# The even block's depthwise convolution as a blockwise real Fourier transform on TensorE, and S5's GpSimd products on VectorE

## The chip, the cores and the metric

The kernel runs on one core of one Trainium2 chip. The metric is the device time of one execution in microseconds (us): the median of several runs. Traces and profile pages come from one further, profiled execution each. TensorE is called PE in the profile's rows (its weight loads PEld), VectorE DVE, ScalarE ACT, GpSimd POOL and SyncE SP.

## The reference

The program is a stack of blocks on 512 tokens of 1024 channels. The change touches only the first one, the even block. After a root-mean-square norm `u` of the input it computes:

```python
p = u @ ev_w_in                                  # 1024 -> 5120
a_in, a_z, b_val, b_gate, b_z = split(p)         # 1024 channels each
ya = gelu(s5_layer(a_in))                        # state-space layer, 64 groups of 16 channels
ya = ya * sigmoid(ya @ s5_w_glu + b_glu) * silu(a_z)
h  = b_val * sigmoid(b_gate)
h  = causal depthwise convolution of h, 31 taps, + conv_b
h  = silu(layer_norm(h))
yb = (h @ conv_w_pw + b_pw) * silu(b_z)
x  = x + rms_norm(concat(ya, yb) @ ev_w_out)
```

All of it is in float32. Products on TensorE are made in three passes of a high and a low part: high by high, low by high, high by low (`passes`, L271 to L273). The halves come from `split`: a copy on ScalarE gives the high part (L227), a subtraction the low part (L230).

## The kernel before, in words

The even block lasts from the start to about 728 us. Channels lie on the 128 partitions, 512 tokens along them. `linear` makes one block of 128 output channels at a time: one weight load by DMA (`wraw`), one copy (`whi`, ACT L227), one subtraction (`wlo`, L230), 24 matmuls of 128x512 into a bank of PSUM (`mm`, three banks), and an epilogue. There are two buffers each for `whi` and `wlo`. The order of instructions on each engine isn't the order of the code: this block alone is built under a scheduler that runs at build time, estimates durations and fixes the order of every engine. On the chip each engine then follows its own list strictly, and waits where a semaphore isn't there yet.

The stages, as the trace shows them:

- **Input blocks and tables** (22 to about 85 us): eight blocks of `a_in`, whose `wlo` subtractions GpSimd makes (`eng=nc.gpsimd`), and S5's tables on VectorE.
- **S5 groups** (`s5_group`, to about 200 us): eight groups of eight. For every pair of S5 groups VectorE makes products and sums (L685, L687, L693, L695), GpSimd two of the products (L686, L694); TensorE transposes and multiplies (L700, L701, L709), beside the 16 blocks of `a_z` and `b_z` and some blocks of the convolution's value and gate.
- **Scan** (`s5_scan`, about 204 to 372 us): 63 steps of four operations of 128x128 on VectorE (L743 to L746). Each step needs the one before; within a step L743 and L744 are free of each other, L745 needs L743, and L746 needs both sums.
- **Convolution**: eight blocks of channels, three ways. Four blocks on ScalarE and GpSimd: for each tap ScalarE scales a shifted copy (L853) and GpSimd adds it (L854). Two on TensorE with diagonal weights, which VectorE builds (L825, 62 high and 62 low tiles). Two on VectorE, one `scalar_tensor_tensor` per tap (L860), held back by hand until the scan's last step. The results go to DRAM (`cv_dr`).
- **Chunks and outputs** of S5 (L731, L761), each 128 small matmuls; the outputs need the scan's last state.
- **glu** (eight blocks, after gelu L903 and splits), with LayerNorm over channels on the reloaded convolution (`layer_norm_apply`) beside it, its silu (L919), the eight pointwise blocks, and the output matrix (16 blocks, to 692 us). Then the block's norm and the next block's first operations.

Of the kernel before, what the change touches and what calls it, by code (L numbers as in the profile page):

```python
# [735 lines left out]
def s5_scan(K, tb, rot, H):  # L736
# [3 lines left out]
    for c in range(1, 64):  # L740
        a = rot.tile([128, 2, G5], F32, name="sa")
        b = rot.tile([128, 2, G5], F32, name="sb")
        tt(out=a, in0=H[:, c - 1], in1=tb["R8"], op=OP.mult)  # L743
        tt(out=b, in0=H[:, c - 1, ::-1], in1=tb["J8"], op=OP.mult)  # L744
        tt(out=a, in0=H[:, c], in1=a, op=OP.add)  # L745
        last = tt(out=H[:, c], in0=a, in1=b, op=OP.add)  # L746
    return last
# [22 lines left out]
def stage_even(K, xt):  # L770
# [9 lines left out]
    with ExitStack() as es:  # L780
        R = pool(es, "evr", 2)
        uh, ul = K.enter(xt, K.rms_pre("norm_pre0"))
        K.xs.close()

# [25 lines left out]
        acc = K.stat("acc")  # L810
        first = []

        def conv_pe(j, hb, c):

            hs = [PE.tile([128, T + 30], F32R, name=n) for n in ("hbh", "hbl")]
            wt = [PE.tile([128, 31], F32R, name=n) for n in ("wth", "wtl")]
            K.split(wt[0], wt[1], K.v("conv_w", j, 241)[:, ::8], eng=nc.gpsimd)
            K.split(hs[0], hs[1], hb, eng=nc.gpsimd)
            ps = K.mm_ps()
            for q0 in range(0, 31, 8):  # L820
                n = min(8, 31 - q0)
                dg = [PE.tile([128, 8, 128], F32R, name=s, bufs=2) for s in ("dgh", "dgl")]
                for a, b in zip(dg, wt):
                    for q in range(n):
                        nc.vector.tensor_scalar(out=a[:, q], in0=K.ident, scalar1=b.bitcast(F32)[:, q0 + q:q0 + q + 1],  # L825
                                                scalar2=None, op0=OP.mult)
                K.passes(ps, [(dg[0][:, q], dg[1][:, q], hs[0][:, q0 + q:q0 + q + T], hs[1][:, q0 + q:q0 + q + T])
                              for q in range(n)], q0 == 0, q0 + n == 31)
            act(out=c, in_=ps, func=AF.Identity, bias=K.v("conv_b", j))

        def conv(j):
            kind = "p" if j in CONV_POOL else "e" if j in CONV_PE else "v"
            P = R if kind == "p" else PE
            hb = P.tile([128, T + 30], F32, name="hb" + kind, bufs=1 if kind == "e" else 2)
            nc.gpsimd.memset(hb[:, 0:30], 0.0)
            sg = R.tile([128, T], F32, name="sg")

            def epi_g(_, ps):
                act(out=sg, in_=ps, func=AF.Sigmoid)

            def epi_v(_, ps):
                nc.vector.tensor_tensor(out=hb[:, 30:], in0=ps, in1=sg, op=OP.mult)

            K.linear(w, [24 + j], uh, ul, epi_g)
            K.linear(w, [16 + j], uh, ul, epi_v)
            c = P.tile([128, T], F32, name="cvt" + kind, bufs=1 if kind == "e" else 2)
            if j in CONV_PE:
                conv_pe(j, hb, c)
            elif j in CONV_POOL:
                act(out=c, in_=hb[:, 0:T], func=AF.Identity, scale=K.v("conv_w", j), bias=K.v("conv_b", j))  # L850
                for q in range(1, 31):
                    t = R.tile([128, T], F32, name="cq")
                    act(out=t, in_=hb[:, q:q + T], func=AF.Copy, scale=K.v("conv_w", 8 * q + j))  # L853
# [1410 lines left out]
```

## Time and profile before

| | before |
|---|---|
| time, median of 3 runs | 4395.85 us (4386.81 to 4398.39) |
| profiled execution | 4396.65 us, span 4394.9 us, mean granted clock 0.967 |
| TensorE busy | 4106.9 us, 93% |
| VectorE busy | 2749.7 us, 63% |
| ScalarE busy | 1754.1 us, 40% |
| GpSimd busy | 766.1 us, 17% |

Rows of the profile read so: line of the kernel, engine, operation, output<-inputs, partitions x elements, count, then busy time and mean ns of one, then the idle time of the engine just ahead of them and what ended it. Rows of a timeline begin with the start and the duration in us. A matmul's recorded duration holds its whole way through the array; the distance between two starts is what TensorE needs for one.

### The profile page before, as it was taken

The page shows a single profiled execution, that of the slowest core. Times are in us where ns is not written, and L with a number is a line of the kernel's source. Part 1 is how long each engine was busy: PE and PEld are TensorE (multiplying, and loading weights), DVE is VectorE, ACT ScalarE, POOL GpSimd, SP SyncE. Part 2 cuts the span into 40 slices and gives each one's busy share as a digit, 9 for nine tenths or more (in the row PEclk, how much of TensorE's full clock was granted, in tenths as well). Part 3 has the DMA queues.
Part 4 walks back from the last instruction along what each step waited for, and adds up shares of the span by engine and source line. Part 5 has one row for each costly group of instructions (what it writes and reads, how often), then busy time and mean ns, then how long its engine had stood idle before and what let it go on. Part 6 is the DMA issues. An engine that isn't in the chain of part 4 may idle for free.

```text
span 4394.9 us, 54853 instructions
## 1 busy us (share of the span) xinstructions
PE 4106.9 (93%) x20700; PEld 3395.0 (77%) x20700; DVE 2749.7 (63%) x5196; ACT 1754.1 (40%) x2785; POOL 766.1 (17%) x746
## 2 busy tenths in 40 slices
PE   7877897999999898999999999999989999999998
PEld 5666676777876687888888888888877788877887
DVE  8999735545453799887665444444546878834334
ACT  3643634443335532444222232323264344444333
POOL 4765201101021333000000000000123222211000
PEclk9988998999999999999999999999999999999999
DMA  5553533334321123456654333434234222343222
GB/s 150 111 125 116 173 103 121 124 106 144 124 69 46 65 78 124 183 206 227 192 193 136 120 122 118 128 115 130 88 125 145 68 71 71 96 143 109 96 97 86
DMA packets 275064, 532.37 MB, mean 121 GB/s; under 512 B 75968, under 2 KB 149568, under 8 KB 271184
## 3 DMA queue, kind: packets, MB, share of 16 engines
q1 hardware_dynamic: 263328, 505.75, 36.4%
q10 hardware_dynamic: 9216, 9.97, 0.8%
q0 software_dynamic: 2256, 13.17, 0.7%
q8 instruction: 162, 2.65, 0.3%
q14 instruction: 102, 0.84, 0.1%
HBM read 438.11 MB, written 90.70 MB: 120 GB/s over the span
## 4 chain that ended last, share of the span: by engine, by line
PE 54%; DVE 11%; issue 3%; ACT 2%; DMA 1%; POOL 1%; DVEq 0%; POOLq 0%; SPq 0%; ACTq 0%
PE mm L271 15%; PE mm L272 15%; PE mm L273 15%; PE ax L1508 3%; PE z L1225 1%; DVE ti L1435 1%; DVE wlo L230 1%; PE ck L2033 1%; DVE ts L1433 1%; DVE bi L1451 1%; DVE wz L1985 0%; DVE bs L1449 0%; PE po L1234 0%; PE z L1207 0%; DVE eq L1463 0%
## 5 line engine op out<-in xcount | busy, mean ns | idle before, releaser
L271 PE MATMUL mm<-uh,whi 128*128 128x512 f32 (+1 forms) x2888 | 1152.0, 400 | 55.3 <-ACT uh L227 23.7
L273 PE MATMUL mm<-uh,wlo 128*128 128x512 f32 (+1 forms) x2888 | 1130.2, 392 | 56.3 <-DVE wlo L230 55.1
L272 PE MATMUL mm<-ul,whi 128*128 128x512 f32 (+1 forms) x2888 | 1130.7, 392 | 11.2 <-DVE ul L230 8.7
L230 DVE TENSOR_TENSOR wlo<-wraw,whi 128x1024 fp32r<-128x1024 f32 x416 | 530.5, 1277 | 520.1 <-ACT whi L227 509.7
L227 ACT ACTIVATE whi<-wraw 128x1024 fp32r<-128x1024 f32 x455 | 480.2, 1057 | 913.5 <-PE mm L272 655.1
L273 PEld LDWEIGHTS mm<-uh,wlo 128*128 128x128 f32 x2888 | 560.4, 194 | 171.7 <-DVE wlo L230 63.7
L271 PEld LDWEIGHTS mm<-uh,whi 128*128 128x128 f32 x2888 | 560.8, 195 | 170.3 <-ACT whi L227 25.9
L272 PEld LDWEIGHTS mm<-ul,whi 128*128 128x128 f32 x2888 | 560.9, 194 | 121.3 <-DVE ul L230 13.7
L272 PE MATMUL mm<-pl,vh 128*128 128x512 f32 (+1 forms) x1056 | 405.8, 384 | 0.3 <-DVE pl L230 0.3
L271 PE MATMUL mm<-ph,vh 128*128 128x512 f32 (+1 forms) x1056 | 394.2, 385 | 7.4 <-ACT ph L227 7.4
L273 PE MATMUL mm<-ph,vl 128*128 128x512 f32 (+1 forms) x1056 | 398.4, 384 | 0.0
L227 ACT ACTIVATE vh<-wraw 128x1024 fp32r<-128x1024 f32 x128 | 132.8, 1058 | 533.1 <-PE mm L272 327.4
L230 DVE TENSOR_TENSOR vl<-wraw,vh 128x1024 fp32r<-128x1024 f32 x128 | 155.4, 1223 | 206.1 <-ACT vh L227 206.1
L1605 DVE TENSOR_TENSOR Y<-mm,Y 128x512 f32<-128x512 f32 (+1 forms) x256 | 164.9, 670 | 142.3 <-PE mm L273 142.2
L1610 POOL COPY acc<-xt 128x256 f32<-128x256 f32 x2 | 1.9, 958 | 1430.7 <-DVE xt L1608 1430.7
L271 PEld LDWEIGHTS mm<-ph,vh 128*128 128x128 f32 x1056 | 200.0, 190 | 47.0 <-ACT ph L227 8.0
L272 PEld LDWEIGHTS mm<-pl,vh 128*128 128x128 f32 x1056 | 199.8, 189 | 39.5 <-DVE pl L230 0.5
L273 PEld LDWEIGHTS mm<-ph,vl 128*128 128x128 f32 x1056 | 199.9, 189 | 38.8
L854 POOL TENSOR_TENSOR cvtp<-cvtp,cq 128x512 f32<-128x512 f32 x120 | 175.3, 1462 | 96.0 <-ACT cq L853 90.8
L272 PE MATMUL mm<-wlo,uh 128*128 128x256 f32 x480 | 139.2, 291 | 2.3 <-DVE wlo L230 2.3
L271 PE MATMUL mm<-whi,uh 128*128 128x256 f32 x480 | 137.6, 291 | 1.2 <-ACT whi L227 0.7
L273 PE MATMUL mm<-whi,ul 128*128 128x256 f32 x480 | 138.2, 289 | 0.0
(1070 smaller groups left out, 7116.9 us busy)
## 6 DMA issues: line engine op xcount, KB each, us to landing
wraw<-in_peer_u_dram SPq DMA_DIRECT2D x128, 512.0 KB, 3.5
wraw<-in_peer_v_dram SPq DMA_DIRECT2D x128, 512.0 KB, 3.6
wraw<-in_w_in_f_dram SPq DMA_DIRECT2D x66, 512.0 KB, 3.4
G_dr<-st SPq DMA_DIRECT2D x16, 2048.0 KB, 7.2
gt<-G_dr SPq DMA_DIRECT2D x32, 1024.0 KB, 6.9
wraw<-in_w_ffn_dram SPq DMA_DIRECT2D x64, 512.0 KB, 3.5
wraw<-in_w_ada_dram SPq DMA_DIRECT2D x48, 512.0 KB, 3.4
wraw<-in_ev_w_in_dram SPq DMA_DIRECT2D x40, 512.0 KB, 3.4
```

Of the source, the lines that this page charges most:

```text
L227: nc.scalar.activation(out=hi, in_=x, func=AF.Copy)
L230: eng.tensor_tensor(out=lo, in0=x, in1=hi.bitcast(F32), op=OP.subtract)
L271: nc.tensor.matmul(ps, ah, bh, start=first and j == 0, stop=False)
L272: nc.tensor.matmul(ps, ah, bl, start=False, stop=False)
L273: nc.tensor.matmul(ps, al, bh, start=False, stop=last and j == n - 1)
L854: nc.gpsimd.tensor_tensor(out=c, in0=c, in1=t, op=OP.add)
L1225: nc.tensor.matmul(ps[b][:, 128 * (c - b):n], ntri if c == b else nones, at(sp, c, wide[c]), start=False, stop=c == 3, skip_group_check=True)
L1433: v.max(out=ts_[:, x, a:b], in_=src[:, x])
L1435: v.max_index(out=ti[:, x, a:b], in_max=ts_[:, x, a:b], in_values=src[:, x])
L1451: v.max_index(out=bi[:, b, a:a + 8], in_max=bs[:, b, h, a:a + 8], in_values=cand[:, b].rearrange("t i j -> t (i j)"))
L1508: nc.tensor.matmul(pg[:, (r % 4) * 128:(r % 4 + 1) * 128], a[:, r], e[:, r], start=True, stop=True)
L1605: tt(out=Y[:, m, ts], in0=ps, in1=Y[:, m, ts], op=OP.add)
```

## The change

- The convolution's value and gate (2048 output channels) come out with tokens on partitions: eight token blocks of 256 channels (`linear_tok`), each with 96 matmuls of 128x256 and two weight loads. Their weights are laid out again on the host, in another argument.
- The convolution is made in overlapping blocks of 128 new and 30 old tokens: a forward real transform (a matrix of 158 rows in two parts, `fw`), a product with the transformed taps (`wh`, L991), the inverse transform (`iv`) with the bias (L995). Both transforms are three-pass matmuls of 128x256 on TensorE. The products and splits are on VectorE and ScalarE. There are four quarters of 256 channels. `conv_tables` builds the matrices and the transformed taps from iotas, polynomials and the taps.
- LayerNorm is over the free dimension (`layer_norm_tok`): reduce on VectorE, squares with sums on ScalarE, one scaling. 32 transposes (L910) bring the channels back to the partitions for silu (L912).
- The pointwise blocks now stand before gelu, glu in the code; before, they stood behind them.
- The two S5 products of GpSimd are VectorE's now, and GpSimd's eight `wlo` subtractions too. The rotating buffers of the groups are two instead of three, the chunk stage works in four parts instead of two, `cv_dr` is gone.

The rest of the program keeps its instructions and their order.

```diff
 def s5_group(K, tb, p1, rot, g0, u, H, G_dr, K_dr):
...
-        nc.gpsimd.tensor_tensor(out=t2, in0=pv(tb["Q2"]), in1=cv(1), op=OP.mult)
+        tt(out=t2, in0=pv(tb["Q2"]), in1=cv(1), op=OP.mult)
...
-        nc.gpsimd.tensor_tensor(out=w2, in0=pw(tb["Q"]), in1=bv(tb["bbi"]), op=OP.mult)
+        tt(out=w2, in0=pw(tb["Q"]), in1=bv(tb["bbi"]), op=OP.mult)
...
-            K.linear(w, range(0, 8), uh, ul, epi_a, eng=nc.gpsimd, front=2)
+            K.linear(w, range(0, 8), uh, ul, epi_a, front=2)
...
-        for j in CONV_ORDER:
-            if isinstance(j, tuple):
-                K.linear(w, zb[j[0]:j[1]], uh, ul, lambda x, ps, j=j: silu_z(x + j[0], ps))
-            else:
-                conv(j)
+        K.linear(w, list(range(16, 24)) + list(range(8, 16)), uh, ul, silu_z)
+        cv = pool(es, "evc", 1).tile([128, KT, T], F32, name="cv")
+        ft = es.enter_context(ExitStack())
+        ct = cv.rearrange("p k t -> p (k t)").rearrange("p (t c) -> p t c", c=D)
+        conv(K, pool(ft, "evx", 2), d["ev_w_t"], uh, ul, fw, iv, wh, ct)
+        layer_norm_tok(K, pool(ft, "evn", 1), ct, 1e-6)
+        for k in range(KT):
+            ps = K.bank("wt")
+            for t in range(4):
+                nc.tensor.transpose(ps[:, t * 128:(t + 1) * 128], ct[:, t, k * 128:(k + 1) * 128], K.ident)
+            s = R.tile([128, T], F32, name="sg")
+            act(out=s, in_=ps, func=AF.Silu, scale=K.v("conv_ln_g", k), bias=K.v("conv_ln_b", k))
+            K.split(uh[:, k], ul[:, k], s)
+        ft.close()
...
+        K.linear(d["conv_w_pw"], range(8), uh, ul, epi_pw)
         s5.close()
...
+def conv(K, X, w, uh, ul, fw, iv, wh, out):
...
+    for q in range(4):
...
+        def epi_g(_, tp, ps):
+            act(out=sg[tp], in_=ps, func=AF.Sigmoid)
+
+        def epi_v(_, tp, ps):
+            h = X.tile([128, 2, 256], F32, name="hv")
+            tt(out=h, in0=ps, in1=sg[tp], op=OP.mult)
+            K.split(hh[:, 2 * tp:2 * tp + 2], hl[:, 2 * tp:2 * tp + 2], h)
+
+        K.linear_tok(w, [4 + q], uh, ul, epi_g)
+        K.linear_tok(w, [q], uh, ul, epi_v)
+        for t in range(4):
+            ps = K.bank("wt").rearrange("p (x c) -> p x c", x=2)
+            for x in range(2):
+                K.passes(ps[:, x], [(fw[0][:, b, x], fw[1][:, b, x], hh[:, t - b], hl[:, t - b])
+                                    for b in range(2 if t else 1)])
+            f = X.tile([128, 2, 256], F32, name="pf")
+            fh, fl = (X.tile([128, 2, 256], F32R, name=n) for n in ("ph", "pl"))
+            tt(out=f, in0=ps, in1=wh[:, :, cs], op=OP.mult)
+            K.split(fh, fl, f)
+            ps = K.bank("wt")[:, :256]
+            K.passes(ps, [(iv[0][:, x], iv[1][:, x], fh[:, x], fl[:, x]) for x in range(2)])
+            tt(out=out[:, t, cs], in0=ps, in1=bias[:, cs], op=OP.add)
+
+
+def layer_norm_tok(K, S, x, eps):
...
+    for t in range(4):
+        nc.vector.tensor_reduce(out=st[:, 0, t:t + 1], in_=x[:, t], axis=AX.X, op=OP.add)
+    nc.vector.tensor_scalar(out=st[:, 0], in0=st[:, 0], scalar1=-1.0 / D, scalar2=None, op0=OP.mult)
+    for t in range(4):
+        sq = K.wp.tile([128, KT, 128], F32, name="wraw", tag="wraw", bufs=3)
+        nc.scalar.activation(out=sq.rearrange("p k n -> p (k n)"), in_=x[:, t], func=AF.Square,
+                             bias=st[:, 0, t:t + 1], accum_out=st[:, 1, t:t + 1])
+    K.rsqrt(st[:, 2], st[:, 1], 1.0 / D, eps, n=4)
+    for t in range(4):
+        nc.vector.tensor_scalar(out=x[:, t], in0=x[:, t], scalar1=st[:, 0, t:t + 1], scalar2=st[:, 2, t:t + 1],
+                                op0=OP.add, op1=OP.mult)
```

Lines of the changed kernel differ: L227 is L230 there, L230 is L233, the passes L271 to L273 are L274 to L276, S5's products L685 to L695 are L763 to L773, the scan's L743 to L746 are L822 to L825, the chunks' L731 is L810, the outputs' L761 is L839, gelu's L903 is L935, and silu's L919 is L912.

Where the order of an engine changes, three places are shown. First VectorE at the start of the S5 groups; `t` and `w` are the products, `Gm` and the last `w` the sums, `fac` and `s5cc`, `bbr`, `bbi` the tables. Before, two products and two sums per pair of groups:

```order
L685 TENSOR_TENSOR t_830<-facP_249,s5cc 128x288
L693 TENSOR_TENSOR w_835<-facP,bbr 128x2x128
L685 TENSOR_TENSOR t_846<-facP_249,s5cc 128x288
L687 TENSOR_TENSOR Gm<-t_830,t_831 128x288
L693 TENSOR_TENSOR w_851<-facP,bbr 128x2x128
L695 TENSOR_TENSOR w_835<-w_835,w_836 128x2x128
L687 TENSOR_TENSOR Gm<-t_846,t_847 128x288
```

The same place after:

```order
L763 TENSOR_TENSOR t_976<-facP_392,s5cc 128x288
L764 TENSOR_TENSOR t_977<-facQ_393,s5cc 128x288
L771 TENSOR_TENSOR w_981<-facP,bbr 128x2x128
L772 TENSOR_TENSOR w_982<-facQ,bbi 128x2x128
L765 TENSOR_TENSOR Gm<-t_976,t_977 128x288
L773 TENSOR_TENSOR w_981<-w_981,w_982 128x2x128
L763 TENSOR_TENSOR t_992<-facP_392,s5cc 128x288
```

L764 and L772 are new on VectorE, so that a pair of groups is six operations there instead of four, and none of them has an input from GpSimd.

Second, VectorE in the scan after the change (`sa`, `sb` and `H` are the scan's, `hv` and `hl` a gated value and its low part, `pf` and `pl` a spectrum and its low part, `cv` the convolved tokens):

```order
L824 TENSOR_TENSOR sa<-H,sa 128x128
L233 TENSOR_TENSOR hl<-hv,hh 128x512
L825 TENSOR_TENSOR H<-sa,sb 128x128
L822 TENSOR_TENSOR sa<-H,R_385 128x128
L823 TENSOR_TENSOR sb<-H,J_386 128x128
L824 TENSOR_TENSOR sa<-H,sa 128x128
L825 TENSOR_TENSOR H<-sa,sb 128x128
```

```order
L824 TENSOR_TENSOR sa<-H,sa 128x128
L991 TENSOR_TENSOR pf<-wt,wh 128x512
L825 TENSOR_TENSOR H<-sa,sb 128x128
L995 TENSOR_TENSOR cv<-wt,cb 128x256
L822 TENSOR_TENSOR sa<-H,R_385 128x128
L823 TENSOR_TENSOR sb<-H,J_386 128x128
L233 TENSOR_TENSOR pl<-pf,ph 128x512
```

The convolution's operations now stand singly between the dependent operations of a step, where before the diagonal weights and weight splits stood.

Third, ScalarE between the LayerNorm and the pointwise blocks after the change (`sg` is silu's output from the transposes in `wt`, `uh` its high part, `ya` gelu's output, `yh` its high part):

```order
L912 ACT_TABLE_LOAD
L912 ACTIVATE sg<-wt,vecs 128x512
L230 ACTIVATE yh<-ya 128x512
L935 ACT_TABLE_LOAD
L935 ACTIVATE ya<-yin_4610 128x8x64
L230 ACTIVATE uh<-sg 128x512
L912 ACT_TABLE_LOAD
L912 ACTIVATE sg<-wt,vecs 128x512
L230 ACTIVATE yh<-ya 128x512
L935 ACT_TABLE_LOAD
```

One silu and one gelu take turns, with a table load ahead of each; before, all eight gelus came well before the first silu of the convolution.

More of the change, by code (lines that the diff above doesn't have):

```diff
@@ L89, in host_layout @@
     lay.add("s5_b_glu", i["s5_b_glu"])
-    lay.add("conv_w", i["conv_w"][0])
-    for n in ("conv_b", "conv_ln_g", "conv_ln_b", "conv_b_pw"):
+    a["conv_w"] = np.ascontiguousarray(i["conv_w"][0])
+    a["conv_b"] = np.ascontiguousarray(i["conv_b"].reshape(1, D))
+    for n in ("conv_ln_g", "conv_ln_b", "conv_b_pw"):
         lay.add(n, i[n])
@@ L718, in s5_chunks @@
     nc = K.nc
-    Tm = p2.tile([128, G5 // 2, 128], F32, name="Tm")
+    n = G5 // 4
+    Tm = p2.tile([128, n, 128], F32, name="Tm")
     nc.gpsimd.memset(Tm, 0.0)
-    for g0 in range(0, G5, G5 // 2):
-        gs = slice(g0, g0 + G5 // 2)
-        u = p2.tile([128, G5 // 2, 64], F32, name="u6")
+    for g0 in range(0, G5, n):
+        gs = slice(g0, g0 + n)
+        u = p2.tile([128, n, 64], F32, name="u6")
         s5_inputs(K, u, A_dr, g0)
@@ L726, in s5_chunks @@
             nc.sync.dma_start(out=Tm[16 * s:16 * s + 16, :, 16 * s:128], in_=K_dr[:, gs, 0:128 - 16 * s])
-        for b in range(0, G5 // 2, 8):
+        for b in range(0, n, 8):
             y = p2.tile([128, 8, 64], F32, name="y5", bufs=2)
@@ L745, in s5_scan @@
         tt(out=a, in0=H[:, c], in1=a, op=OP.add)
-        last = tt(out=H[:, c], in0=a, in1=b, op=OP.add)
-    return last
+        tt(out=H[:, c], in0=a, in1=b, op=OP.add)
 def s5_outputs(K, rot, q, H, G_dr, Y1_dr, Y_dr):
@@ L808, in stage_even @@
             s5_outputs(K, rot, q, H, G_dr, Y1_dr, Y_dr)
[L810 to L853, printed above, removed]
-                    nc.gpsimd.tensor_tensor(out=c, in0=c, in1=t, op=OP.add)
-            else:
-                with K.tc.issue_after(scan.ins):
-                    nc.vector.tensor_scalar(out=c, in0=hb[:, 0:T], scalar1=K.v("conv_w", j),
-                                            scalar2=K.v("conv_b", j), op0=OP.mult, op1=OP.add)
-                for q in range(1, 31):
-                    nc.vector.scalar_tensor_tensor(
-                        out=c, in0=hb[:, q:q + T], scalar=K.v("conv_w", 8 * q + j),
-                        in1=c, op0=OP.mult, op1=OP.add)
-            if not first:
-                first.append(j)
-                nc.gpsimd.tensor_copy(out=acc, in_=c)
-            else:
-                nc.gpsimd.tensor_tensor(out=acc, in0=acc, in1=c, op=OP.add)
-            nc.gpsimd.dma_start(out=cv_dr[:, j], in_=c)
@@ L912, in stage_even @@
         K.linear(d["s5_w_glu"], range(8), yh, yl, epi_glu)
-        pe.close()
-        cv = pool(es, "evc", 1).tile([128, KT, T], F32, name="cv")
-        nc.sync.dma_start(out=cv, in_=cv_dr)
-        layer_norm_apply(K, cv, acc, 1e-6)
-        for k in range(KT):
-            s = R.tile([128, T], F32, name="sg")
-            act(out=s, in_=cv[:, k], func=AF.Silu, scale=K.v("conv_ln_g", k), bias=K.v("conv_ln_b", k))
-            K.split(uh[:, k], ul[:, k], s)
-        def epi_pw(j, ps):
-            nc.vector.scalar_tensor_tensor(
-                out=cv[:, j], in0=ps, scalar=K.v("conv_b_pw", j), in1=load_z(j), op0=OP.add, op1=OP.mult)
-        K.linear(d["conv_w_pw"], range(8), uh, ul, epi_pw)
         for k in range(KT):
```

115 lines of the change are left out of this document (88 added, 27 removed).

## The prediction

> **What bounds the kernel now.** The program is one chain of stages, and the order of instructions on each engine is the same before and after from 728 us on. So I read the page's slices first, then the even stage by windows.
>
> ```profile
> span 4394.9 us, 54853 instructions
> DVE  8999735545453799887665444444546878834334
> POOL 4765201101021333000000000000123222211000
> PEclk9988998999999999999999999999999999999999
> ```
>
> One slice is 110 us. In slices 2 to 4 VectorE is at 90% or more, GpSimd at 50 to 70% up to slice 4, and TensorE's granted clock is 0.8 in slices 3 and 4. The windows show the same per stage: S5 groups to 200 us, scan to 372, outputs and the rest of the convolution to 483, glu, LayerNorm and pointwise to 601, output matrix to 692.
>
> ```profile
> 22.00:200.00 178.00, 155.03 (x774) 117.34 (x774) 170.18 (x283) 89.93 (x128) 119.11 (x110) 0.92 0.45 111
> 200.00:372.00 172.00, 119.93 (x511) 97.48 (x511) 164.66 (x304) 78.73 (x112) 107.52 (x86) 0.82 0.52 109
> 372.00:483.00 111.00, 93.14 (x417) 76.26 (x417) 107.49 (x184) 48.74 (x60) 46.91 (x32) 0.87 0.53 155
> 483.00:601.00 118.00, 111.23 (x457) 87.45 (x458) 67.54 (x83) 62.48 (x83) 22.14 (x16) 0.96 0.47 155
> 601.00:692.00 91.00, 90.25 (x439) 75.56 (x437) 27.52 (x31) 28.29 (x39) 0.00 (x0) 1.00 0.28 93
> ```
>
> The columns after the length are busy time of PE, its weight loads, DVE, ACT and POOL, then the clock. To 483 us VectorE is busy 96% of the time and sets the pace; behind it TensorE does. "Busy" flatters TensorE, since records overlap and lengthen at the lower clock. Its true need comes from start-to-start distances at full clock:
>
> ```profile
> 607.37 0.39 PE L271 MATMUL mm<-uh,whi 128*128 128x512 f32 x1
> ...
> 611.92 0.39 PE L273 MATMUL mm<-uh,wlo 128*128 128x512 f32 x1
> 864.45 0.28 PE L271 MATMUL mm<-whi,uh 128*128 128x256 f32 x1
> ...
> 865.89 0.28 PE L271 MATMUL mm<-whi,uh 128*128 128x256 f32 x1
> 385.94 3.72 PE L761 MATMUL ax<-H,Gm 128*128 128x63 f32 x32
> ```
>
> Twenty steps from 607.37 to 611.92 give 0.2275 us for 128x512; twelve from 864.45 to 865.89 give 0.12 for 128x256; 3.72/32 is about 0.115 for a small S5 matmul. The stage has 72 projection blocks of 24 passes (393 us), 186 convolution passes (42) and 576 S5 matmuls (66): 501 us of work in the 670 us from 22 to 692. So 169 us are lost to waits and to the low clock that follows them. By the same count per window 48, 71, 31, 15 and 3 us are lost: nearly all of it under the busy VectorE.
>
> Why VectorE is slow there is seen in the groups (lines, engine, form, count | busy, mean ns) and in one stretch of the scan:
>
> ```profile
> L854 POOL TENSOR_TENSOR cvtp<-cvtp,cq 128x512 f32<-128x512 f32 x120 | 175.3, 1462 | 96.0 <-ACT cq L853 90.8
> L860 DVE SCALAR_TENSOR_TENSOR cvtv<-hbv,vecs,cvtv 128x512 f32<-128x512 f32 x60 | 57.1, 977 | 0.0
> L743 DVE TENSOR_TENSOR sa<-H,R 128x128 f32<-128x128 f32 x63 | 42.5, 674 | 9.5 <-ACT H L713 7.6
> L746 DVE TENSOR_TENSOR H<-sa,sb 128x128 f32<-128x128 f32 x63 | 41.3, 655 | 1.9
> L745 DVE TENSOR_TENSOR sa<-H,sa 128x128 f32<-128x128 f32 x63 | 39.4, 625 | 0.0
> L744 DVE TENSOR_TENSOR sb<-H,J 128x128 f32<-128x128 f32 x63 | 18.9, 299 | 0.0
> L685 DVE TENSOR_TENSOR t<-facP,s5cc 128x288 f32<-128x288 f32 x32 | 27.1, 847 | 0.2
> L825 DVE TENSOR_SCALAR dgl<-ident,wtl 128x128 fp32r<-128x128 f32 x62 | 25.1, 461 | 0.0
> L825 DVE TENSOR_SCALAR dgh<-ident,wth 128x128 fp32r<-128x128 f32 x62 | 20.6, 394 | 1.1 <-PE mm L272 1.1
> ```
>
> ```profile
> 230.42 0.29 DVE L743 TENSOR_TENSOR sa<-H,R 128x128 f32<-128x128 f32 x1
> ...
> 231.47 0.29 DVE L743 TENSOR_TENSOR sa<-H,R 128x128 f32<-128x128 f32 x1
> ...
> 234.74 1.33 DVE L743 TENSOR_TENSOR sa<-H,R 128x128 f32<-128x128 f32 x1
> ```
>
> ```profile
> 233.25 4.17 POOL L854 TENSOR_TENSOR cvtp<-cvtp,cq 128x512 f32<-128x512 f32 x3 [3.75 <-ACT cq L853]
> ```
>
> While GpSimd waits, one scan step takes 231.47 − 230.42 = 1.05 us; beside a GpSimd addition the same L743 takes 1.33 instead of 0.29. All 63 steps sum to 42.5 + 41.3 + 39.4 + 18.9 = 142 us, against 63 × 1.05 = 66 clean. The Trainium skill ("SBUF — State Buffer", Who interferes with whom) says that a VectorE instruction with two SBUF inputs and a GpSimd one that reads SBUF lock each other out for a whole instruction; the 1.33 beside the 0.29 agrees.
>
> **The change part by part.** *TensorE's work.* 56 blocks stay (56 × 24 × 0.2275 = 306); the 16 value and gate blocks become 8 token blocks of 96 passes of 128x256 (768 × 0.12 = 92); the convolution becomes 264 passes of that form (32); S5 keeps 66; transposes and table matmuls add some 5. That is 501 again: the change gives TensorE nothing directly. Whatever it brings is lost time that goes.
>
> *GpSimd.* L854 (175 us) and the S5 products leave. What remains on GpSimd in the stage is DMAs, fills and eight late products.
>
> *VectorE, S5 groups.* 64 products come over. Clean prices of the neighbours:
>
> ```profile
> 92.34 0.45 DVE L687 TENSOR_TENSOR Gm<-t,t 128x288 f32<-128x288 f32 x1
> 92.71 0.41 DVE L693 TENSOR_TENSOR w<-facP,bbr 128x256 f32<-128x256 f32 x1
> 93.05 0.45 DVE L685 TENSOR_TENSOR t<-facP,s5cc 128x288 f32<-128x288 f32 x1
> ```
>
> Starts 0.37 and 0.34 apart: six operations for each of 32 pairs are 32 × (3 × 0.37 + 3 × 0.34) = 68 us, with the weight splits (some 16 × 1.14, a row below) 86. At L685's slow mean (0.85) for each of the 192 it would be 163, 180 with the splits. I take the clean one, since the partner that slows them is the one removed. Convolution tables, 13.5 us by their element counts, and eight weight splits of L230 move ahead of the groups, which start near 85 us.
>
> *VectorE, the scan.* 66 us of steps, 15 weight splits (17), and three quarters of the new convolution's operations.
>
> ```profile
> 504.69 4.91 DVE L952 TENSOR_TENSOR cv<-cv,mu 128x512 f32<-128x512 f32 x8 [2.69 <-DMA cv<-cv_dr]
> ...
> 510.12 1.22 DVE L230 TENSOR_TENSOR wlo<-wraw,whi 128x1024 fp32r<-128x1024 f32 x1
> 511.25 0.68 DVE L909 TENSOR_TENSOR sg<-sg,ya 128x512 f32<-128x512 f32 x1
> ```
>
> A weight split takes 511.25 − 510.12 = 1.13 from start to start (1.14 above and below). One 128x512 operation is 4.91/8 = 0.61: 8 products, 8 splits, 16 spectrum products, 16 splits at that and 16 bias additions at about 0.34 are 35 us, so 26 here. Sum 109 us. Gone are L860's 57 us and the 25.1 + 20.6 of the diagonal weights.
>
> *Queues.* SyncE now loads the chunk stage's strips in four rounds for two, 32 more transfers, and no longer reads back the 2 MB of convolution output.
>
> ```profile
> wraw<-in_ev_w_in_dram SPq DMA_DIRECT2D x40, 512.0 KB, 3.4
> ```
>
> I cost the rounds at nothing: token passes stand between the chunk groups in TensorE's order and cover them. Uncovered, two more rounds would show two landings like this one's, 7 us.
>
> **Timeline after.** (a) To the end of the groups TensorE has 8 A and 16 z blocks (131), 320 S5 matmuls (37), tables and the first gate passes (9): 177, more than VectorE's 86 past 85 us, so it decides. Of the 48 us lost there before I keep half, 24, for the start-up, the tables and the low clock after gaps: end at 22 + 177 + 24 = 223. (b) Then the remaining token passes (85), three quarters of the convolution (24), chunks and outputs (29): 138, over VectorE's 109. Each token block uses both weight buffers, so the next waits for a split; I price that at 10 in all: 371. (c) The last quarter's chain product, split, forward, product, split, inverse ends 13 us later; LayerNorm's sums, squares and root take 10; then ScalarE must run all eight silus before the pointwise matmuls can finish. Its new order alternates silu with S5's gelu: 12 table loads, 8 silus, 6 gelus, 13 copies.
>
> ```profile
> 466.01 1.28 ACT L872 ACT_TABLE_LOAD   x1
> 467.30 0.60 ACT L872 ACTIVATE sg<-mm 128x512 f32<-128x512 f32 x1
> 467.92 1.28 ACT L903 ACT_TABLE_LOAD   x1
> ...
> 469.21 1.18 ACT L903 ACTIVATE ya<-yin 128x512 f32<-128x512 f32 x1
> 470.42 0.63 ACT L227 ACTIVATE yh<-ya 128x512 fp32r<-128x512 f32 x1
> ```
>
> ```profile
> L919 ACT ACTIVATE sg<-cv,vecs 128x512 f32<-128x512 f32 x8 | 6.3, 810 | 2.2 <-DVE ul L230 1.8 <-POOL ya L910 0.3
> ```
>
> 12 × 1.28 + 8 × 0.81 + 6 × 1.18 + 13 × 0.63 = 37. So (c) is 60 us, in which TensorE has only transposes and two pointwise blocks: before, this LayerNorm lay beside glu and cost nothing; now glu stands behind it and covers nothing. End at 431. (d) Six pointwise blocks (33), glu (44), output matrix (91 as before) and about 6 for the refilled pipeline and clock: 605. Before it was 692, so 87 us are won. On the profiled run's 4396.65 (its span 4394.9, 0.8 above the median 4395.85) that gives 4310.
>
> A rule speaks against (c). A load in the trace starts at 466.01, and the next operation at 467.30, 1.29 later; the one ahead is not delayed. The Trainium skill ("ScalarE: Activation LUTs", What ACT_TABLE_LOAD costs) puts a switch at about 2.7 us with the drain of the engine; by it the estimate for the twelve would be 17 us more, 4327. The trace agrees with the load's part and shows none of the drain's.
>
> **The rivals.** *The stage closes up.* The groups run at TensorE's pace with 8 lost instead of 24, no waits in (b), and the silu chain overlaps more, 40 for 60: 46 more, 4264. For it: VectorE has 37 us to spare in (b). Against: the LayerNorm needs every channel first. 15%.
>
> *The scan stays late.* TensorE's order puts the first S5 output matmuls inside the last value block, and they need the last scan step. If each step's four dependent operations, interleaved with convolution operations, take 1.9 us, the scan lasts 63 × 1.9 + 43 = 163 past 223, to 386; the outputs, 29 us of the work of (b) and the passes queued behind them, then come some 25 late, and with 15 more in the groups about 40 of the 87 are gone: 4350. 19%.
>
> *The switch is dearer.* If a switch in alternation costs twice its load, as a drain beside the load would, (c) grows by 12 × 1.28 = 15: 4325. The five rows above speak against it. The Trainium skill's drain, cited above, would be this case. 4%.
>
> *Slower.* If VectorE's operations have slow means for a reason of their own and not GpSimd's, its work sets the end: groups 180 past 85 (265), scan 142, splits 17 and the 26 of the convolution at L860's 0.98 for 0.61 (42), to 466, (c) a tenth longer (to 532), (d) 174: 706, or 14 behind: 4411. It decides if VectorE's work grows by more than the 87 us won. Against it stands the 1.05 us step. 4%.
>
> **How the numbers follow.** The forecast case has 58%, and its own range is ±25 us (the 24, 10 and 60). The range runs from the closing-up case, 4264 less a few, to the late scan plus 10: 4258 to 4360. It leaves out the slower case and tails. A measurement of this kernel can tell about 0.3% (13 us). Faster 0.93, within 0.3% 0.03 (the worst of the late scan), slower 0.04.
>
> **What would show it.** Right: scan rows L822 to L825 all near 0.29 and about 1.05 us a step; TensorE's gap-free stretches with a clock over 0.9 to the end of the groups; an idle TensorE of 40 us between the last value block and the pointwise blocks, released by ScalarE's uh; the output matrix ending near 605. Wrong: scan operations over 0.5 us with an idle GpSimd; output matmuls waiting for the scan; the table loads gone or at twice their length; a stage after 728 that changes its length.

## The result, and the profile after

The changed kernel takes 4324.65 us (median of four runs, 4315.6 to 4329.3), the kernel before 4395.2 us in the same session: a ratio of 0.9843, 95% interval 0.983 to 0.9856, or 70.5 us less. The forecast was 4310. The profiled execution took 4320.94 us with a span of 4319.2, 75.7 less than before's span.

The slices of the page, to hold against those of before:

```profile
DVE  8675445545636699886664444444637888734334
POOL 1000001101211441000000000000123222211000
PEclk9997999999999999999999999999999999999999
```

GpSimd's slices 2 to 6 are empty, VectorE's slices 2 to 4 are at 60%, 70% and 50% instead of over 90%, and the low clock is one slice, the fourth: about 325 to 430 us. The windows of the even block, cut at the ends of its stages (columns as before):

```profile
22.00:223.00 201.00, 195.63 (x1035) 155.79 (x1036) 154.34 (x419) 90.92 (x129) 14.99 (x20) 0.99 0.53 142
223.00:360.00 137.00, 134.31 (x1086) 133.36 (x1085) 108.02 (x322) 36.49 (x51) 0.00 (x0) 0.96 0.51 124
360.00:375.00 15.00, 11.25 (x75) 11.11 (x75) 5.94 (x9) 1.78 (x3) 0.00 (x0) 0.77 0.84 217
375.00:436.00 61.00, 31.43 (x126) 22.32 (x124) 27.50 (x41) 42.92 (x54) 0.00 (x0) 0.67 0.49 158
436.00:615.00 179.00, 173.52 (x776) 141.17 (x776) 66.83 (x76) 64.56 (x83) 10.72 (x8) 0.97 0.36 113
```

To 360 us TensorE is busy 98% of the time at a clock of 0.96 to 0.99. From 375 us on come 61 us in which it works half the time at 0.67: the LayerNorm and the silus. The output matrix ends at 614 us, where before it ended at 692. The scan's four lines and two of the groups', from the lines of the block:

```profile
L825 DVE TENSOR_TENSOR H<-sa,sb 128x128 f32<-128x128 f32 x63 | 18.2, 289 | 1.5
L822 DVE TENSOR_TENSOR sa<-H,R 128x128 f32<-128x128 f32 x63 | 18.2, 289 | 11.2 <-ACT H L791 9.7
L823 DVE TENSOR_TENSOR sb<-H,J 128x128 f32<-128x128 f32 x63 | 17.9, 284 | 0.0
L824 DVE TENSOR_TENSOR sa<-H,sa 128x128 f32<-128x128 f32 x63 | 17.9, 284 | 0.0
L763 DVE TENSOR_TENSOR t<-facP,s5cc 128x288 f32<-128x288 f32 x32 | 14.6, 455 | 24.6 <-PE wt L778 24.4
L764 DVE TENSOR_TENSOR t<-facQ,s5cc 128x288 f32<-128x288 f32 x32 | 14.5, 452 | 0.0
```

The scan's operations sum to 72 us instead of 142, and VectorE now waits for TensorE in the groups (24.4 us, L763); before, TensorE waited there for VectorE (15.5 us from 85 to 200 us, for L695). The stretch that stays open, TensorE's part of the timeline; the brackets are idle time and what ended it:

```profile
385.24 0.58 PE L274 MATMUL wt<-ph,ivh 128*128 128x256 f32 x1 [2.74 <-ACT ph L230]
400.81 2.98 PE L910 MATMUL wt<-ident,cv 128*128 128x128 f32 x12 [13.40 <-DVE cv L1011]
...
426.32 1.22 PE L274 MATMUL mm<-uh,whi 128*128 128x512 f32 x2 [2.54 <-ACT uh L230]
431.79 0.73 PE L274 MATMUL mm<-uh,whi 128*128 128x512 f32 x2 [2.54 <-ACT uh L230]
437.25 1.22 PE L274 MATMUL mm<-uh,whi 128*128 128x512 f32 x2 [2.99 <-ACT uh L230]
```

The LayerNorm's scaling (L1011) ends 13.4 us of idleness, then one `uh` after the other lets matmuls through; the last three come some 5.5 us apart.

### The profile page after: what moved, and what is told of

It reads as the page before. It is cut to its first block, busy times and chain, and to the rows that moved or that the text cites. A ratio compares the mean times of both kernels' runs of the same rounds, so it can differ in the third digit from the quotient of the medians.

```text
span 4319.2 us, 55373 instructions
## 1 busy us (share of the span) xinstructions
PE 4082.0 (95%) x21200; PEld 3401.0 (79%) x21200; DVE 2572.0 (60%) x5187; ACT 1692.3 (39%) x2693; POOL 496.6 (11%) x529
## 4 chain that ended last, share of the span: by engine, by line
PE 55%; DVE 11%; issue 3%; ACT 2%; POOL 1%; DMA 1%; SPq 0%; DVEq 0%; POOLq 0%; ACTq 0%
PE mm L274 15%; PE mm L275 15%; PE mm L276 15%; PE ax L1563 3%; PE z L1280 1%; DVE ti L1490 1%; DVE wlo L233 1%; PE ck L2088 1%; DVE ts L1488 1%; DVE bi L1506 1%; DVE wz L2040 0%; DVE bs L1504 0%; PE po L1289 0%; PE z L1262 0%; DVE w L1493 0%
## 5 line engine op out<-in xcount | busy, mean ns | idle before, releaser
L274 PE MATMUL mm<-uh,whi 128*128 128x512 f32 (+1 forms) x2760 | 1091.9, 397 | 55.1 <-ACT uh L230 27.5
L276 PE MATMUL mm<-uh,wlo 128*128 128x512 f32 (+1 forms) x2760 | 1072.0, 389 | 18.4 <-DVE wlo L233 17.7
L275 PE MATMUL mm<-ul,whi 128*128 128x512 f32 (+1 forms) x2760 | 1073.1, 389 | 11.0 <-DVE ul L233 8.4
L233 DVE TENSOR_TENSOR wlo<-wraw,whi 128x1024 fp32r<-128x1024 f32 x424 | 533.1, 1259 | 541.0 <-ACT whi L230 530.4
L230 ACT ACTIVATE whi<-wraw 128x1024 fp32r<-128x1024 f32 x455 | 480.4, 1058 | 914.4 <-PE mm L275 649.7
L274 PEld LDWEIGHTS mm<-uh,whi 128*128 128x128 f32 x2760 | 530.4, 193 | 166.0 <-ACT uh L230 30.4
L276 PEld LDWEIGHTS mm<-uh,wlo 128*128 128x128 f32 x2760 | 531.1, 192 | 124.3 <-DVE wlo L233 23.6
L275 PEld LDWEIGHTS mm<-ul,whi 128*128 128x128 f32 x2760 | 531.5, 193 | 113.5 <-DVE ul L233 12.9
L274 PE MATMUL mm<-ph,vh 128*128 128x512 f32 (+1 forms) x1056 | 393.1, 384 | 7.5 <-ACT ph L230 7.5
L276 PE MATMUL mm<-ph,vl 128*128 128x512 f32 (+1 forms) x1056 | 397.4, 383 | 0.0
L230 ACT ACTIVATE vh<-wraw 128x1024 fp32r<-128x1024 f32 x128 | 132.9, 1058 | 528.0 <-PE mm L275 323.5
L233 DVE TENSOR_TENSOR vl<-wraw,vh 128x1024 fp32r<-128x1024 f32 x128 | 155.4, 1224 | 200.5 <-ACT vh L230 191.9
L274 PEld LDWEIGHTS mm<-ph,vh 128*128 128x128 f32 x1056 | 199.1, 189 | 46.9 <-ACT ph L230 8.1
L276 PEld LDWEIGHTS mm<-ph,vl 128*128 128x128 f32 x1056 | 198.6, 188 | 38.8
L275 PE MATMUL mm<-wlo,uh 128*128 128x256 f32 x736 | 212.5, 290 | 3.3 <-DVE wlo L233 3.2
L274 PE MATMUL mm<-whi,uh 128*128 128x256 f32 x736 | 209.7, 290 | 1.7 <-DVE kb L1381 1.0
L276 PE MATMUL mm<-whi,ul 128*128 128x256 f32 x736 | 210.9, 288 | 0.0
L275 PEld LDWEIGHTS mm<-wlo,uh 128*128 128x128 f32 x736 | 142.6, 194 | 8.0 <-DVE wlo L233 4.6
```

The costliest lines, as they stand in the source:

```text
L230: nc.scalar.activation(out=hi, in_=x, func=AF.Copy)
L233: eng.tensor_tensor(out=lo, in0=x, in1=hi.bitcast(F32), op=OP.subtract)
L274: nc.tensor.matmul(ps, ah, bh, start=first and j == 0, stop=False)
L275: nc.tensor.matmul(ps, ah, bl, start=False, stop=False)
L276: nc.tensor.matmul(ps, al, bh, start=False, stop=last and j == n - 1)
```

## The experiments

Each ratio below is against the kernel before, measured in the same session; the changed kernel's is 0.9843.

**Was it GpSimd that slowed VectorE?** Additions on GpSimd whose result nothing uses, beside the scan of the changed kernel:

```diff
         tt(out=H[:, c], in0=a, in1=b, op=OP.add)
+        if c == 1:
+            d = [rot.tile([128, 512], F32, name=f"du{j}", bufs=1) for j in range(2)]
+            for x in d:
+                nc.gpsimd.memset(x, 0.0)
+            nc.gpsimd.tensor_copy(out=d[0][:, 0:128], in_=H[:, 1].rearrange("p z g -> p (z g)"))
+            for _ in range(80):
+                nc.gpsimd.tensor_tensor(out=d[0], in0=d[0], in1=d[1], op=OP.add)
```

> The changed kernel with 80 additions of 128x512 on GpSimd, of scratch data that nothing uses, started by the scan's first step. My theory (the two engines lock each other out): the scan's operations L822, L824 and L825 go from 0.29 to about 0.6 to 0.7 in the mean, the scan from 122 us to 180 to 200, S5's outputs and the last quarter of the convolution come 55 to 75 us later, time 4375 to 4400. Rival (the scan was slow before for reasons of its own, as operations interleaved between dependent ones): the operations stay at 0.29, time within 5 us of the changed kernel.

Measured: 4396.31 us, ratio 1.001 (1.0001 to 1.002). The whole gain is gone. The additions and the scan in this kernel:

```profile
L832 POOL TENSOR_TENSOR du<-du,du 128x512 f32<-128x512 f32 x80 | 112.7, 1409 | 6.3
```

```profile
L822 DVE TENSOR_TENSOR sa<-H,R 128x128 f32<-128x128 f32 x63 | 43.3, 687 | 11.2 <-ACT H L791 9.7
L825 DVE TENSOR_TENSOR H<-sa,sb 128x128 f32<-128x128 f32 x63 | 43.0, 682 | 1.5
L824 DVE TENSOR_TENSOR sa<-H,sa 128x128 f32<-128x128 f32 x63 | 42.1, 668 | 0.0
L823 DVE TENSOR_TENSOR sb<-H,J 128x128 f32<-128x128 f32 x63 | 17.9, 284 | 0.0
```

The means are close to before's (0.674, 0.655, 0.625, 0.299 there), and the last step begins at 414 us instead of 344. They are means of two kinds of step: the additions run only to 346 us. L822 up to then and after it, in the source view (count, then duration as minimum, median and maximum in ns, then the first and last start):

```profile
L822 DVE TENSOR_TENSOR sa<-H,R x27: 293/1311/1362, 225.6 to 343.6; 128x128 f32<-128x128 f32 x27
L822 DVE TENSOR_TENSOR sa<-H,R x36: 281/291/295, 347.7 to 414.1; 128x128 f32<-128x128 f32 x36
```

Beside the additions the operation takes 1.3 us at the median, and behind the last of them 0.29 again. The order on VectorE, ScalarE and TensorE in the even block is that of the changed kernel but for one small fill, so GpSimd's work alone makes the difference. L823, which needs no result of the scan operation ahead of it, keeps its 0.284.

**The same from the other side:** the kernel before without most of GpSimd's taps. The convolution is not computed fully here, so only the time counts.

```diff
-                for q in range(1, 31):
+                for q in range(1, 2):
                     t = R.tile([128, T], F32, name="cq")
```

> The kernel before with 29 of the 30 GpSimd additions (and ScalarE's scaled copies for them) left out in each of the four blocks that GpSimd convolves, so the convolution is not computed fully; all other work as before. Theory (the loss was VectorE locked out by GpSimd): the scan's operations fall to 0.29, the scan from 168 us to 90 to 110, and 60 to 90 us of the 670 up to the output matrix go: 4305 to 4335, though TensorE's restructured convolution isn't there. Rival (the loss was the place of VectorE's other work, the diagonal weights and its own taps, between the scan's steps): less than 25 us, 4370 to 4395.

Measured: 4300.93 us, ratio 0.9796 (0.9779 to 0.9813): 93 us less, somewhat more than my theory allowed, though nothing of TensorE's new convolution is in it. The scan lasts 112 us instead of 168. Its lines:

```profile
L743 DVE TENSOR_TENSOR sa<-H,R 128x128 f32<-128x128 f32 x63 | 20.5, 326 | 5.8 <-ACT H L713 4.0
L746 DVE TENSOR_TENSOR H<-sa,sb 128x128 f32<-128x128 f32 x63 | 19.3, 306 | 1.9
L744 DVE TENSOR_TENSOR sb<-H,J 128x128 f32<-128x128 f32 x63 | 17.9, 284 | 0.0
L745 DVE TENSOR_TENSOR sa<-H,sa 128x128 f32<-128x128 f32 x63 | 17.9, 284 | 0.0
```

Together the two runs show what the change gains from: GpSimd's additions put back beside the scan take the whole gain away, and leaving the taps out brings as much and more. This run also takes ScalarE's scaled copies away, its LayerNorm still lies beside glu, and the scheduler made a new order for it; all of that is in its 93 us, and it wasn't separated.

**What the S5 products are worth, in both kernels.** First the changed kernel with them back on GpSimd:

```diff
-        tt(out=t2, in0=pv(tb["Q2"]), in1=cv(1), op=OP.mult)
+        nc.gpsimd.tensor_tensor(out=t2, in0=pv(tb["Q2"]), in1=cv(1), op=OP.mult)
...
-        tt(out=w2, in0=pw(tb["Q"]), in1=bv(tb["bbi"]), op=OP.mult)
+        nc.gpsimd.tensor_tensor(out=w2, in0=pw(tb["Q"]), in1=bv(tb["bbi"]), op=OP.mult)
```

> The changed kernel with S5's two products per pair back on GpSimd, all else as changed. My theory: TensorE, not VectorE, sets the end of the groups now (VectorE idles a quarter of the time there), so slower group operations on VectorE (0.7 to 0.9 us instead of 0.42 to 0.46) are covered: time within 10 us of the changed kernel, 4315 to 4335 us, and the scan's operations stay at 0.29. Rival: it is the S5 part of the change that frees VectorE and TensorE; then the groups end some 20 to 40 us later and the time is 4345 to 4365.

Measured: 4334.84 us, ratio 0.9874 (0.9857 to 0.9891), at the upper edge of what my theory allowed. The scan begins at 223.6 us, as without the edit (223.3), so the groups don't end later. That they are covered was hardly put to the test: VectorE's operations there take 0.48 to 0.71 us in the mean, less than I expected, and with 64 products fewer it is busy for 94 us from 85 to 223 us in both kernels. The loss is elsewhere: the order made for this program puts two rounds of ScalarE's issues of S5's output transfers in a row, ahead of the last quarter's copies.

```profile
353.60 15.88 ACTq L843 DMA_DIRECT2D Y_dr<-y  x8
369.52 0.63 ACT L230 ACTIVATE hh<-hv 128x512 fp32r<-128x512 f32 x1 [17.81 <-DMA Y_dr<-y]
```

ScalarE stands 17.8 us there; the last bias addition starts at 395.0 us instead of 387.4. Not all of the 17.8 us is a loss, and most of it is the issuing itself, not a wait for the data. The second round of four (of `y` from L841), its last issue alone, and the product that the copy needs (L979):

```profile
360.56 0.68 DVE L841 TENSOR_TENSOR y<-ax,y 128x504 f32<-128x504 f32 x1 [3.35 <-PE ax L839]
361.27 8.20 ACTq L843 DMA_DIRECT2D Y_dr<-y  x4
369.16 0.31 ACTq L843 DMA_DIRECT2D Y_dr<-y  x1
361.65 0.69 DVE L979 TENSOR_TENSOR hv<-mm,sg 128x512 f32<-128x512 f32 x1 [0.41 <-PE mm L276]
```

The data of the round is there at 361.2 us, and its first issue follows at once; the four issues themselves take until 369.5. `hv` is ready at 362.3, so the copy is 7.2 us late.

Second, the kernel before with the products, and GpSimd's eight weight subtractions, on VectorE:

```diff
-        nc.gpsimd.tensor_tensor(out=t2, in0=pv(tb["Q2"]), in1=cv(1), op=OP.mult)
+        tt(out=t2, in0=pv(tb["Q2"]), in1=cv(1), op=OP.mult)
...
-        nc.gpsimd.tensor_tensor(out=w2, in0=pw(tb["Q"]), in1=bv(tb["bbi"]), op=OP.mult)
+        tt(out=w2, in0=pw(tb["Q"]), in1=bv(tb["bbi"]), op=OP.mult)
...
-            K.linear(w, range(0, 8), uh, ul, epi_a, eng=nc.gpsimd, front=2)
+            K.linear(w, range(0, 8), uh, ul, epi_a, front=2)
```

> The kernel before with S5's two products and the eight weight subtractions of GpSimd on VectorE, the convolution as before. Theory: VectorE set the pace there, GpSimd goes on adding taps beside it, so VectorE only gets more work (64 products of 0.35 to 0.85 us): the groups end 10 to 35 us later, time 4400 to 4430. Rival: the two products' waits between GpSimd and VectorE were a cost of their own, and this part alone wins: below 4380.

Measured: 4382.97 us, ratio 0.9984 (0.9974 to 0.9995). Neither was right: no slowing, and a gain of some 7 us by the ratio, smaller than the rival asked. GpSimd's and VectorE's taps in the source view, of this kernel, then of before:

```profile
L854 POOL TENSOR_TENSOR cvtp<-cvtp,cq x120: 1262/1341/9814, 91.5 to 409.4; 128x512 f32<-128x512 f32 x120
L860 DVE SCALAR_TENSOR_TENSOR cvtv<-hbv,vecs,cvtv x60: 731/742/1776, 396.9 to 465.7; 128x512 f32<-128x512 f32 x60
```

```profile
L854 POOL TENSOR_TENSOR cvtp<-cvtp,cq x120: 1260/1364/2360, 114.8 to 453.9; 128x512 f32<-128x512 f32 x120
L860 DVE SCALAR_TENSOR_TENSOR cvtv<-hbv,vecs,cvtv x60: 732/743/1786, 373.5 to 481.7; 128x512 f32<-128x512 f32 x60
```

The scan does end 21 us later. But GpSimd starts its taps 23 us earlier and is through 45 us earlier. VectorE's own taps then run beside a mostly idle GpSimd, and end 16 us earlier. The early start isn't GpSimd's own: in both kernels its first tap follows ScalarE's first scaled copy (L853, at 90.7 us here, 114.0 before), so the order made for this program brings it forward. How much of the 45 us is that order, and how much the products that GpSimd no longer makes, wasn't separated; my theory had left out both.

**The exposed chain.** The changed kernel with the gelus held behind the last silu:

```diff
-            act(out=s, in_=ps, func=AF.Silu, scale=K.v("conv_ln_g", k), bias=K.v("conv_ln_b", k))
+            silu = act(out=s, in_=ps, func=AF.Silu, scale=K.v("conv_ln_g", k), bias=K.v("conv_ln_b", k))
...
-            act(out=ya[:, k].rearrange("p (c s) -> p s c", s=8), in_=y, func=AF.Gelu_apprx_tanh)
+            with K.tc.issue_after(silu.ins):
+                act(out=ya[:, k].rearrange("p (c s) -> p s c", s=8), in_=y, func=AF.Gelu_apprx_tanh)
```

> The changed kernel with the gelus held back until the last silu of the convolution's branch, so that they no longer take turns. My theory: the 36 us from the LayerNorm's end to the last uh lie on the path, ScalarE sets them, and without 10 table loads (12.8 us), 6 gelus (6.8) and 5 copies (3.1) they come down to some 14; the gelus then run beside the pointwise blocks. Time some 20 us lower, about 4305. Rival: the stretch is set by transposes, the low parts on VectorE or weight loads, or the later gelus now delay glu by as much: within 5 us of the changed kernel.

Measured: 4302.89 us, ratio 0.9797 (0.9782 to 0.9812), 22 us less than the changed kernel by the medians. One turn on ScalarE in the changed kernel, and the same silus here:

```profile
406.98 1.28 ACT L935 ACT_TABLE_LOAD   x1
408.27 1.16 ACT L935 ACTIVATE ya<-yin 128x512 f32<-128x512 f32 x1
409.22 0.64 ACT L230 ACTIVATE uh<-sg 128x512 fp32r<-128x512 f32 x1
409.88 1.28 ACT L912 ACT_TABLE_LOAD   x1
411.17 0.78 ACT L912 ACTIVATE sg<-wt,vecs 128x512 f32<-128x512 f32 x1
```

```profile
408.00 0.76 ACT L912 ACTIVATE sg<-wt,vecs 128x512 f32<-128x512 f32 x1
408.80 0.63 ACT L230 ACTIVATE uh<-sg 128x512 fp32r<-128x512 f32 x1
409.40 0.78 ACT L912 ACTIVATE sg<-wt,vecs 128x512 f32<-128x512 f32 x1
410.21 0.63 ACT L230 ACTIVATE uh<-sg 128x512 fp32r<-128x512 f32 x1
```

A silu with its copy takes 1.4 us here, against 5.5 with a turn. The last `uh` is there at 418 us instead of 437, though a table load and two gelus still stand ahead of it.

**ScalarE's transfers.** Half of S5's output transfers move to GpSimd's queue:

```diff
-        (nc.sync if t % 2 else nc.scalar).dma_start(
+        (nc.sync if t % 2 else nc.gpsimd).dma_start(
             out=Y_dr[g0 * 16:(g0 + GO) * 16, t, :].rearrange("(g p) c -> p g c", p=16),
```

> The changed kernel with the half of S5's output transfers that ScalarE issues issued by GpSimd instead. My theory: ScalarE stands at these transfers, waiting for the outputs, with the convolution's copies of the last quarter queued behind them; the last quarter's tail, 28 us from its last value pass to its last bias addition in the changed kernel, becomes some 8 us shorter, time about 4316. Rival: the outputs' own chain or TensorE's in-order list holds the tail as long: within 3 us of the changed kernel.

Measured: 4320.88 us, ratio 0.9839 (0.982 to 0.9859): the time can't tell it from the changed kernel. The trace can: the last bias addition starts at 382.1 us instead of 387.4.

```profile
L995 DVE TENSOR_TENSOR cv<-wt,cb x16: 413/424/426, 255.8 to 382.1; 128x256 f32<-128x256 f32 x16
```

The waits are real, but they are worth 5 us there, not 8; `hv` and the spectra on VectorE end ScalarE's idle time once the transfers don't. With gelu_after_silu the same edit was run again:

> The changed kernel with the gelus behind the last silu and ScalarE's half of S5's output transfers on GpSimd's queue. Theory: the two are separate, 22 and 4 us, about 4298. Rival: no better than gelu_after_silu alone, 4303.

Measured: 4297.2 us, ratio 0.979 (0.9777 to 0.9804), the fastest complete version of the study. It is 5.7 us below gelu_after_silu by the medians of two sessions, but the intervals of the ratios overlap, so by the times the second part is likely and not shown.

**Filling TensorE's hole.** Five z blocks behind the LayerNorm:

```diff
-        K.linear(w, list(range(16, 24)) + list(range(8, 16)), uh, ul, silu_z)
+        K.linear(w, list(range(16, 24)) + list(range(8, 11)), uh, ul, silu_z)
...
         layer_norm_tok(K, pool(ft, "evn", 1), ct, 1e-6)
+        K.linear(w, range(11, 16), uh, ul, lambda j, ps: silu_z(11 + j, ps))
```

> The changed kernel with five of the 16 z blocks put behind the LayerNorm in the code, ahead of the transposes. My theory: TensorE sets the pace to the end of the last value block, and has nothing to do for some 28 us after it; five blocks (27 us) taken from the groups and put into that hole end everything some 20 us earlier. In this order the convolution's silus also stand in one piece (the gelus take turns with the z blocks' silus), which is worth up to 15 more. Time 4285 to 4305. Rival: with less beside them the groups are set by VectorE, or the z blocks' silus hold up ScalarE's LayerNorm and silus: within 8 us of the changed kernel, 4317 to 4333.

Measured: 4334.9 us, ratio 0.9867 (0.9851 to 0.9882): worse than the changed kernel. The outputs of S5 and the convolution's silus of this kernel, and the window in which the groups end:

```profile
L839 PEld LDWEIGHTS ax<-H,Gm x128: 187/192/338, 338.5 to 366.8; 128*128 128x128 f32 x128
L913 ACT ACTIVATE sg<-wt,vecs x8: 769/776/780, 435.8 to 448.2; 128x512 f32<-128x512 f32 x8
```

```profile
200.00:225.00 25.00, 15.77 (x97) 12.26 (x95) 12.83 (x42) 12.66 (x16) 2.35 (x2) 0.80 0.50 95
```

Of 27 us of matmuls taken away, the outputs come only 9 earlier (their last start is 375.6 in the changed kernel): TensorE now waits at the groups' end for ScalarE, 9 us in this window, at a clock of 0.80. So TensorE's work alone doesn't set the groups; the waits suggest a chain over TensorE and ScalarE close behind it, which no run isolates. And the z blocks' silus and the gelus now stand ahead of the convolution's, which begin at 435.8 instead of 403.4. Together with the other two edits:

> The changed kernel with five late z blocks, the gelus behind the last silu, and S5's output transfers off ScalarE, together. Theory: the hole of TensorE and the silu chain are two separate losses, 20 and 22 us, and the transfers 4: about 4280. Rival: they are the same loss seen twice, so that together they bring no more than gelu_after_silu did alone, about 4300.

Measured: 4320.8 us, ratio 0.9838 (0.9823 to 0.9852), 18 us more than gelu_after_silu alone. Late z blocks cost in both; neither theory had that.

**glu ahead of the pointwise blocks**, as before the change (the loop of transposes and silus and the pointwise `linear` move behind glu's):

```diff
-        K.linear(d["conv_w_pw"], range(8), uh, ul, epi_pw)
...
         K.linear(d["s5_w_glu"], range(8), yh, yl, epi_glu)
+        for k in range(KT):
+            ps = K.bank("wt")
...
+        K.linear(d["conv_w_pw"], range(8), uh, ul, epi_pw)
```

> The changed kernel with glu ahead of the transposes, silus and pointwise blocks in the code, as it stood before the change; on ScalarE all eight gelus then come ahead of the silus, without turns. Theory (the exposed LayerNorm and silu chain, 50 us from the last bias addition to the last uh, is the largest loss left, because glu covers nothing): glu's 44 us of matmuls run beside LayerNorm's end, and some 15 us before glu and 12 after it stay open: 30 to 40 us less than the changed kernel, 4285 to 4295, and below gelu_after_silu's 4303. Rival: gelu's inputs come from S5's outputs through DRAM too late, so glu starts no earlier than the pointwise blocks did: 4315 to 4330.

Measured: 4302.4 us, ratio 0.98 (0.9787 to 0.9813): 22 us less, not 30 to 40, and no better than gelu_after_silu.

```profile
408.24 1.22 PE L274 MATMUL mm<-yh,whi 128*128 128x512 f32 x2 [5.50 <-ACT yh L230]
```

glu starts at 408 us, not at 402: gelu waits 7.7 us for its input from VectorE. The rival's lateness is half there. Taking the transfers off ScalarE as well moved that start to 402.8:

> The same, with ScalarE's half of S5's output transfers on GpSimd's queue. Theory: the last quarter's copies are no longer behind them, and gelu's inputs come no later: 4 to 8 us less than glu_first, 4278 to 4290. Rival: GpSimd's transfers land later than ScalarE's did, and now gelu waits for them: no gain, or some us more.

Measured: 4301.3 us, ratio 0.9802 (0.9789 to 0.9816): the time can't tell it from glu_first, and the 4278 to 4290 of my theory were missed.

**Differences of a few us.** The last addition to `xt` (L485) ends the even block. It is the last start of these rows, of the changed kernel, then with gelu_after_silu, y_by_gpsimd_queue, both of these edits, and glu_first:

```profile
L485 DVE TENSOR_TENSOR xt<-xt,cv x8: 411/414/945, 622.0 to 636.9; 128x256 f32<-128x256 f32 x8
L485 DVE TENSOR_TENSOR xt<-xt,cv x8: 410/413/945, 602.8 to 617.7; 128x256 f32<-128x256 f32 x8
L485 DVE TENSOR_TENSOR xt<-xt,cv x8: 408/414/942, 615.4 to 630.7; 128x256 f32<-128x256 f32 x8
L485 DVE TENSOR_TENSOR xt<-xt,cv x8: 410/412/946, 595.2 to 610.2; 128x256 f32<-128x256 f32 x8
L485 DVE TENSOR_TENSOR xt<-xt,cv x8: 410/412/946, 611.4 to 624.7; 128x256 f32<-128x256 f32 x8
```

By the end of the block gelu_after_silu gains 19 us, the transfers 6, both together 27, and glu_first 12. From there to the end of the span the same five executions need between 3680 and 3689 us, in a part that no edit touches, so a few us in a time say little. Each row is of a single execution, but by them the two edits add up within the block, and glu_first, equal to gelu_after_silu by the medians, gains less there.

## Why the prediction came out right

*The cause.* VectorE's operations fell to the clean prices: 0.289 and 0.284 in the scan, 0.455 in the groups. That GpSimd's additions were the partner in the scan is shown by gpsimd_busy_in_scan and before_one_tap, from both sides; for the groups no run separates the taps from the products. The Trainium skill ("SBUF — State Buffer", Who interferes with whom) says the same of two-input operations; this case agrees for three of the scan's four, with 1.3 us beside an addition and 0.29 without, and not for L823.

*Stage (a), end at 223.* The scan's first operation starts at 223.3. The number was right, the reason only in part. The 24 us kept for start-up, tables and the low clock were a guess, half of what was lost before, and that they fit is luck: TensorE is idle for only 5.4 of the 201 us, at a clock of 0.99. By the distances between starts the 320 S5 matmuls take some 43 us, not 37, so part of the 24 is work that the sum had too small. And z_late shows that TensorE's work isn't the only bound there.

*Stage (b), 371.* S5's last output matmuls start at 375.6. The scan and what lies in it lasted 122 us, from 223 to 345; VectorE was busy for 102.5 of them, close to the 109 of the sum, and TensorE for 119.4, so TensorE set the pace as forecast. The first output matmul starts at 346.5 without a wait for the scan. Most of the 4 to 5 us are lost behind it, in one wait of the output matmuls (L839) for `Gm` from DRAM, 3.75 us up to 365.5, which the sum didn't have.

*Stage (c), 60 us to 431.* The last bias addition starts at 387.4, the LayerNorm took 13.4 us for 10, the silu chain 36.4 for 37. It ended at 437.2. The twelve table loads were there at 1.28 each, and the gelu at 408.27 starts 1.29 after its load; no drain shows, so the dearer switch didn't happen. The page "ScalarE: Activation LUTs" of the Trainium skill, section What ACT_TABLE_LOAD costs, gives 2.7 us with it; the measurement decides here.

*Stage (d), 174.* Some 177 us, to 614.

So 78 of the 87 us were won by the end of the output matrix: (b) is 4 or 5 us late, the LayerNorm 3, (d) 3. No step failed; these terms were each sized a little small. By the span 75.7 remain, and by the medians 70.5: the profiled run lies 3.7 us under its own median, and before's 1.4 over its own.

*The rivals.* Closing up didn't come: VectorE's spare time didn't shorten (b), and the LayerNorm stayed bare. The late scan didn't come: it had 1.9 us for the four operations of a step and 43 us of other work on top, 163 us in all, and the 122 us measured, 1.9 a step, hold both. The slower case needed VectorE to be slow by itself, which it isn't.

## What to carry to other kernels

Before an operation's mean is used as its price, look for rows of the same operation with the other engine idle: the difference, 142 us against 72 measured here, is what work on that other engine costs, and leaving that work out once, or adding some that nothing uses, measures it. When a stage moves, ask what it had beside it: the LayerNorm was free beside glu and 50 us long bare, and on ScalarE two functions that take turns cost 22 us that a fixed order gave back. Where a scheduler fixes the order, an edit also makes a new order: in before_s5_on_vector the taps came forward, and in s5_on_gpsimd two rounds of issues fell ahead of a copy.

## What the runs showed of the hardware

A transfer can hold the engine that issues it, even when its data is there. Of the rounds of four that ScalarE issues in the changed kernel and in s5_on_gpsimd, the last one starts only 0.2 to 0.5 us before the round's first transfer lands, wherever the trace has that landing: in the round shown above at 369.16 us, where the first transfer, issued at 361.27, takes 8.0 us to land. On GpSimd's queue the issues of a round follow each other every 0.56 us. What makes ScalarE's last one wait wasn't tried. The page shows such a wait as one for the DMA, though the copy behind it needs nothing of it and is late because of the order.

Four operations of the same form lengthen differently beside GpSimd: in gpsimd_busy_in_scan L822, L824 and L825 go to 0.67 to 0.69 us in the mean, and L823, which follows L822 at once, stays at 0.284 (0.38 at most). In the kernel before, the same operation (L744) was lengthened now and then, with a mean of 0.299 and at most 1.38. Why it is spared wasn't tried.
